# Layer-norm factors folded into the weight splits, early loads in another order and on other queues, compression later

## Chip, cores and metric

The kernel runs on one core of one Trainium2 chip. The metric is the device time of one execution in microseconds (us).

## What is computed

Two layers over 256 tokens of width 1024, in float32. Each layer normalises x by its root mean square with a gain per channel, projects it with one combined matrix, feeds three groups of heads from the result, adds their output projection to x, and then adds a squared-ReLU MLP behind a second norm.

```python
def rms_norm(x, gain):
    y = x * lax.rsqrt(jnp.mean(x * x, -1, keepdims=True) + NORM_EPS) * gain
...
for l in range(DEPTH):                                   # 2 layers
    proj = rms_norm(x, ln1_gain[l]) @ w_in[l]            # 1024 -> 2866 columns
    # split into: NSA q, k_cmp, v_cmp, k_slc, v_slc, k_win, v_win, gates; MLA cq, ckv, kpe; retention q, k, v, gate
    o_nsa = nsa_mixer(...)        # 6 heads: compressed, selected and window branch, gated
    o_mla = mla_mixer(...)        # 5 heads, low-rank keys and values
    o_ret = retention_mixer(...)  # 5 heads, two chunks of 128
    x = x + concat(o_nsa, o_mla, o_ret) @ w_out[l]
    h = rms_norm(x, ln2_gain[l])
    x = x + jnp.square(jax.nn.relu(h @ w_up[l])) @ w_down[l]   # width 4096
return rms_norm(x, final_gain)
```

The compressed branch adds position rows to blocks of 32 keys (values), multiplies each flattened block by `cmp_w1` (2048 x 128), applies gelu and multiplies by `cmp_w2`.

## The kernel before

**Products in three passes.** TensorE works on float32r. Every weight and every activation is held as two parts, `hi` (a rounded copy, made by ScalarE, L140) and `lo` (the remainder, made by VectorE, L141), and `mm3` adds three products (L146 to L148). A weight must be loaded, split, and only then multiplied.

**The stream of weights.** Class `Stream` holds all weights in the order of their use, in units of up to 128 x 1024. A unit is loaded by SP into one of `RAW` = 5 raw buffers, then split into one of `SPL` = 5 pairs of `hi` and `lo`. `get` loads up to `LOAD_AHEAD` = 12 units ahead and splits up to `SPLIT_AHEAD` = 4 ahead. The raw buffer is free again when the split is done. The four `w1` units of the compression are used as loaded: they keep their raw buffers until TensorE has read them. `PIECES` says into how many pieces a split is cut; `START_POOL` names two units of the first chunk whose remainders GpSimd makes.

**Order of a layer.** `inproj` projects chunk by chunk: A (gates and the latent vectors of MLA, 434 columns), B2 (k_cmp, v_cmp, k_slc), B1 (queries), B3 (v_slc, k_win, v_win), of 384 columns each, and rq, rk, rg, rv of the retention, 320 each. Each chunk adds 8 slices of 128 channels for 2 tiles of 128 tokens into two accumulators (tag `acc`, two buffers); ScalarE takes them out with the norm's factor per token, `rstd`, a power that GpSimd computes (L194). In the program the compression (`ps_h`, 64 products with `w1`, then gelu and `ps_kc`) stands between B2 and B1. Then come NSA's scores (`ps_s`), values, retention, the output projection (`l_po`) and the MLP (`ps_up`, `l_pd`). The engines' order is laid by a planner from simulated times: `PRIO` moves parts ahead of or behind their place, and loads go wherever they fit into a queue's planned time, so a load for layer 1 can stand in SP's queue early in layer 0.

**The norm.** `norm_half` multiplies half a tile of x by the gain (`xg`; on GpSimd for one tile of tokens, on VectorE for the other, L503; for the first layer behind the transposes, L499), transposes it on TensorE with the identity (in `c0s`) and splits the result into `xT`. Gains for all later norms are rows broadcast to 128 partitions by SP (512 KB each).

**Small loads.** Per layer SP issues two loads of the MLA norms (L363, L364), two of `w2` and sixteen of position rows (L402, L404), and one of the retention gain (L151). The mask array `c1s` (1056 KB) is one load. GpSimd issues a single load, the positions (L181).

Of the kernel before, what the change touches and what calls it, by code (L numbers as in the profile page):

```python
# [7 lines left out]
F32 = mybir.dt.float32  # L8
# [14 lines left out]
# column offsets of the combined input projection  # L23
# [3 lines left out]
# columns of the first constant array  # L27
C_ID, C_INV, N_C0 = 0, 128, 176
# columns of the second one
C_TRI, C_CM, C_VALID, C_BLK, C_DEC, C_FOLD, N_C1 = 0, 384, 416, 417, 801, 2081, 2113  # L30

# units of weights that are held as loaded and as split; units loaded and split ahead of their use
RAW, SPL, LOAD_AHEAD, SPLIT_AHEAD = 5, 5, 12, 4

# the order of the token tiles where the attention ends
TORD = (1, 0)

# products that only raise the tensor engine's clock before the inputs arrive
WARM = 8
# how far ahead of its place in the program the scheduler takes each part of the work  # L40
# [14 lines left out]
def _parts():  # L55
    """2*pi times 2**11 and 2*pi, cut into parts whose products with small integers are exact."""
# [21 lines left out]
def tile_hybrid_trunk(  # L78
# [59 lines left out]
    def split(hi, lo, src, eng=nc.vector):  # L138
        """src = hi + lo, with hi and lo as the tensor engine's one-pass type."""
# [3 lines left out]

    def mm3(o, a, b, start, stop):
        """o += a^T b in three passes of the operands' parts."""
# [7 lines left out]
    # ---------------------------------------------------------------- inputs that stay  # L153
# [7 lines left out]
    def load_gain(key, row):  # L161
        g = p2.tile([P, D], F32, name=f"gain_{key}", tag="gain", bufs=1)
# [3 lines left out]
    g8 = p2.tile([8, P], F32, name="g8", tag="gain", bufs=1)  # L166
    nc.sync.dma_start(c0s, c0)
    nc.sync.dma_start(xs[:, 0, 0:512], xv[:, 0, 0:512])
# [999 lines left out]
```

## Time and profile before

| | |
|---|---|
| time, median of 3 runs | 682.01 us (680.02 to 683.09) |
| span of the profiled execution | 679.9 us |
| TensorE products / weight loads busy | 659.6 us (97%) / 582.3 us (86%) |
| VectorE busy | 426.9 us (63%) |
| ScalarE busy | 378.4 us (56%) |
| GpSimd busy | 67.2 us (10%) |
| mean granted TensorE clock | 0.992 |
| moved | 111.64 MB, 164 GB/s over the span |

The span runs from the first to the last instruction of one profiled execution; the shortest of the three runs is 0.1 us longer, the median 2.1 us. Products are pipelined and their ends are modelled, so TensorE's busy time says that it had work, not that it ran at its peak.

### The profile page before, as it was taken

The numbers are of one execution on the slowest core, as the hardware profiler recorded it, in microseconds if no ns is written. First come the engines' busy times: TensorE is split into PE (matmuls) and PEld (weight loads), VectorE is DVE, ScalarE is ACT, GpSimd is POOL, SyncE is SP. The second block draws the span as 40 slices with busy tenths as digits, with TensorE's granted clock in tenths as the row PEclk, the third lists the DMA queues.
The fourth block names the chain that finished last, engine by engine and source line by source line (L and its number), as shares of the span: only waits on it lengthen the run. The fifth ranks groups of instructions, "written<-read, shape, count | busy, mean of one in ns | idle before, by whom it ended". The sixth has DMA issues, their size and how long they took to land.

```text
span 679.9 us, 11370 instructions
## 1 busy us (share of the span) xinstructions
PE 659.6 (97%) x4151; PEld 582.3 (86%) x4151; DVE 426.9 (63%) x987; ACT 378.4 (56%) x855; POOL 67.2 (10%) x116
## 2 busy tenths in 40 slices
PE   7989999999999999999999999999999999999995
PEld 5978988677989898989889998876698898989894
DVE  6755867776755555555585597677685555555554
ACT  5856776363745454545466786636284545454542
POOL 3420401201000000000023132111100000000000
PEclk9998899999999999999999999999999999999998
DMA  7897634222865656565647584331285655555511
GB/s 225 254 194 238 176 108 118 71 63 94 281 188 165 208 169 212 166 208 174 180 128 200 168 244 133 93 94 42 83 270 182 199 179 195 185 188 185 186 63 62
DMA packets 79512, 111.64 MB, mean 164 GB/s; under 512 B 9432, under 2 KB 67680, under 8 KB 79328
## 3 DMA queue, kind: packets, MB, share of 16 engines
q1 hardware_dynamic: 79424, 110.92, 53.1%
q8 instruction: 32, 0.52, 0.3%
q14 instruction: 24, 0.20, 0.1%
q0 software_dynamic: 32, 0.00, 0.0%
HBM read 109.86 MB, written 1.05 MB: 163 GB/s over the span
## 4 chain that ended last, share of the span: by engine, by line
PE 88%; DMA 5%; DVE 3%; ACT 2%; issue 1%; SPq 0%; POOL 0%; POOLq 0%; ACTq 0%
PE ps_up L146 9%; PE ps_up L147 9%; PE ps_up L148 9%; PE l_pd L147 8%; PE l_pd L148 8%; PE l_pd L146 8%; DMA raw_B<-in_w_in_dram 3%; PE l_po L146 2%; PE l_po L148 2%; PE l_po L147 2%; PE l_oT L855 2%; PE ps_pT L863 1%; PE ps_s L146 1%; PE l_B L146 1%; DMA raw_rk<-in_w_in_dram 1%; PE l_B L147 1%
## 5 line engine op out<-in xcount | busy, mean ns | idle before, releaser
L141 DVE TENSOR_TENSOR lo_wd<-raw_wd,hi_wd 128x1024 fp32r<-128x1024 f32 x64 | 78.2, 1225 | 111.3 <-ACT hi_wd L140 111.1
L146 PE MATMUL ps_up<-xT,lo_wu 128*128 128x256 f32 x512 | 144.9, 283 | 1.3 <-ACT xT L140 1.3
L147 PE MATMUL ps_up<-xT,hi_wu 128*128 128x256 f32 x512 | 144.9, 283 | 0.0
L148 PE MATMUL ps_up<-xT,hi_wu 128*128 128x256 f32 x512 | 144.1, 282 | 0.0
L140 ACT CAST hi_wd<-raw_wd 128x1024 fp32r<-128x1024 f32 x64 | 67.1, 1051 | 113.7 <-PE l_pd L148 68.0
L148 PE MATMUL l_pd<-hi_wd,u_h 128*128 128x512 f32 x256 | 100.2, 391 | 0.0
L147 PE MATMUL l_pd<-lo_wd,u_h 128*128 128x512 f32 x256 | 100.1, 391 | 0.0
L146 PE MATMUL l_pd<-hi_wd,u_l 128*128 128x512 f32 x256 | 99.7, 389 | 0.0
L140 ACT CAST hi_wu<-raw_wu 128x512 fp32r<-128x512 f32 x128 | 72.6, 618 | 46.3 <-PE ps_up L148 39.0
L146 PEld LDWEIGHTS ps_up<-xT,lo_wu 128*128 128x128 f32 x512 | 96.0, 187 | 2.8 <-ACT xT L140 1.8
L147 PEld LDWEIGHTS ps_up<-xT,hi_wu 128*128 128x128 f32 x512 | 96.3, 188 | 1.4 <-DVE xT L141 0.4
L148 PEld LDWEIGHTS ps_up<-xT,hi_wu 128*128 128x128 f32 x512 | 97.1, 190 | 0.0
L141 DVE TENSOR_TENSOR lo_wu<-raw_wu,hi_wu 128x512 fp32r<-128x512 f32 x128 | 82.1, 685 | 24.0 <-ACT hi_wu L140 23.9
L148 PEld LDWEIGHTS l_pd<-hi_wd,u_h 128*128 128x128 f32 x256 | 48.0, 188 | 10.1
L147 PEld LDWEIGHTS l_pd<-lo_wd,u_h 128*128 128x128 f32 x256 | 48.0, 188 | 9.5
L146 PEld LDWEIGHTS l_pd<-hi_wd,u_l 128*128 128x128 f32 x256 | 48.1, 188 | 9.4
L141 DVE TENSOR_TENSOR lo_B<-raw_B,hi_B 128x192 fp32r<-128x192 f32 (+1 forms) x80 | 28.7, 414 | 24.4 <-ACT hi_B L140 24.2
L146 PE MATMUL l_B<-hi_B,xT 128*128 128x384 f32 x96 | 33.1, 353 | 2.8 <-ACT q_sb L569 2.8
L140 ACT CAST hi_B<-raw_B 128x192 fp32r<-128x192 f32 (+1 forms) x80 | 25.1, 381 | 18.9 <-DMA raw_B<-in_w_in_dram 14.4
L148 PE MATMUL l_B<-hi_B,xT 128*128 128x384 f32 x96 | 32.6, 340 | 0.0
L147 PE MATMUL l_B<-lo_B,xT 128*128 128x384 f32 x96 | 32.5, 339 | 0.0
L819 ACT ACTIVATE p_nsa<-p_nsa,nsa_m 128x256 f32<-128x256 f32 (+2 forms) x72 | 28.4, 397 | 3.3 <-DVE nsa_m L817 3.0
(322 smaller groups left out, 1252.0 us busy)
## 6 DMA issues: line engine op xcount, KB each, us to landing
raw_wu<-in_w_up_dram SPq DMA_DIRECT2D x64, 512.0 KB, 4.6
raw_wd<-in_w_down_dram SPq DMA_DIRECT2D x64, 512.0 KB, 4.2
raw_B<-in_w_in_dram SPq DMA_DIRECT2D x24, 384.0 KB, 3.7
raw_wo<-in_w_out_dram SPq DMA_DIRECT2D x10, 512.0 KB, 3.7
raw_A<-in_w_in_dram SPq DMA_DIRECT2D x8, 434.0 KB, 5.1
raw_wo<-in_w_out_dram SPq DMA_DIRECT2D x12, 256.0 KB, 3.7
raw_w<-in_cmp_w_k_dram SPq DMA_DIRECT2D x8, 256.0 KB, 6.4
raw_w<-in_cmp_w_v_dram SPq DMA_DIRECT2D x8, 256.0 KB, 6.1
```

What stands on the lines that cost most here:

```text
L140: a = nc.scalar.copy(out=hi, in_=src)
L141: b = eng.tensor_tensor(lo, src, hi.bitcast(F32), op=ALU.subtract)
L146: nc.tensor.matmul(o, a[1], b[0], start=start, stop=False)
L147: nc.tensor.matmul(o, a[0], b[1], start=False, stop=False)
L148: nc.tensor.matmul(o, a[0], b[0], start=False, stop=stop)
L819: nc.scalar.activation(p[:, o:o + n], p[:, o:o + n], AF.Exp, scale=-1.0, bias=ms[:, r, b:b + 1], accum_out=ls[:, r, b:b + 1])
L855: nc.tensor.matmul(oT[gp, 0:384], kv_sb[kt][:, vi, gp], pTs[g][:, 0:384], start=i == 0, stop=False)
L863: last = nc.tensor.transpose(ps[:, r * P:(r + 1) * P], prs[g][:, r, o:o + P], ident)
```

## The change

- The gains of both norms are no longer multiplied into x. All four rows of gains are loaded once (`g32`), transposed to one column per slice of 128 channels (`gT`), and multiplied into the weights while these are split: `split_gain` makes `hi` by a ScalarE activation with a factor per partition and `lo` by one VectorE instruction with two operations. Since the factor changes with the slice of channels, each split is cut by slices: 8 pieces a chunk of `w_in`, 4 pieces of 256 columns a unit of `w_up` (before: 2 of 512). `norm_half` keeps the transposes and the split of x. The three broadcast loads of gains go; the final gain is loaded behind the last weights.
- The constants and `g32` are loaded on ScalarE's queue; SP loads the left halves of both tiles of x, then two units of A, then the right halves. B2's first unit comes ahead of the MLA weights.
- The MLA norms, `w2`, the position rows and the retention gain are loaded on GpSimd's queue. The mask array comes in two loads.
- The compression (its products and the loads of `w1`) stands behind rq, and rq ahead of NSA.
- GpSimd no longer splits weights, the rotary tables stand behind chunk A, and `RAW` is 6.

```diff
-RAW, SPL, LOAD_AHEAD, SPLIT_AHEAD = 5, 5, 12, 4
+RAW, SPL, LOAD_AHEAD, SPLIT_AHEAD = 6, 5, 12, 4
...
-PIECES = {'A': 2, 'B1': 4, 'B2': 2, 'B3': 4, 'rk': 2, 'rg': 4, 'rv': 2, 'wo': 2, 'wu': 2}
-START_POOL = (1, 2)
+PIECES = {'wo': 2}
...
+    def split_gain(hi, lo, src, g):
+        nc.scalar.activation(hi, src, AF.Copy, scale=g)
+        nc.vector.scalar_tensor_tensor(lo, in0=src, scalar=g, in1=hi.bitcast(F32), op0=ALU.mult, op1=ALU.subtract)
...
-        g = p2.tile([P, D], F32, name=f"gain_{key}", tag="gain", bufs=1)
+        g = p1.tile([P, D], F32, name=f"gain_{key}", tag="mid")
...
-    nc.sync.dma_start(c0s, c0)
-    nc.sync.dma_start(xs[:, 0, 0:512], xv[:, 0, 0:512])
-    nc.sync.dma_start(g8, ln1_gain[0].rearrange("(k p) -> k p", p=P))
-    nc.sync.dma_start(xs[:, 0, 512:D], xv[:, 0, 512:D])
+    g32 = p2.tile([32, P], F32, name="g32", tag="h_sb", bufs=1)
+    nc.scalar.dma_start(c0s, c0)
+    nc.scalar.dma_start(g32[0:16], ln1_gain.rearrange("l (k p) -> (l k) p", p=P))
+    nc.scalar.dma_start(g32[16:32], ln2_gain.rearrange("l (k p) -> (l k) p", p=P))
+    for t in range(2):
+        nc.sync.dma_start(xs[:, t, 0:512], xv[:, t, 0:512])
...
     def late_start():
-        nc.sync.dma_start(xs[:, 1, :], xv[:, 1, :])
+        for t in range(2):
+            nc.sync.dma_start(xs[:, t, 512:D], xv[:, t, 512:D])
...
+            if parts:
+                for g, a, b in parts:
+                    split_gain(p[0][:, a:b], p[1][:, a:b], raw[:, a:b], gT[:, g:g + 1])
+                return p
...
-                     nc.gpsimd if (l, name) == (0, "A") and i in START_POOL else nc.vector)
+                     [(8 * l + k, j * n, (j + 1) * n) for j, k in enumerate(ks)])
...
-            nc.sync.dma_start(nrm[:, 0:2], mla_q_norm[l].rearrange("(k p) -> p k", p=P))
-            nc.sync.dma_start(nrm[:, 2:3], mla_kv_norm[l].rearrange("(k p) -> p k", p=P))
+            nc.gpsimd.dma_start(nrm[:, 0:2], mla_q_norm[l].rearrange("(k p) -> p k", p=P))
+            nc.gpsimd.dma_start(nrm[:, 2:3], mla_kv_norm[l].rearrange("(k p) -> p k", p=P))
...
-                nc.sync.dma_start(w2s[:, z], w2[l])
+                nc.gpsimd.dma_start(w2s[:, z], w2[l])
                 for rep in range(8):
-                    nc.sync.dma_start(pos_t[rep * 16:(rep + 1) * 16, z], pe[l].rearrange("(b a) d -> a b d", b=2))
+                    nc.gpsimd.dma_start(pos_t[rep * 16:(rep + 1) * 16, z], pe[l].rearrange("(b a) d -> a b d", b=2))
...
-                                    wuv[:, 4 * i:4 * i + 4, c * 256:(c + 1) * 256])], 1024)
+                                    wuv[:, 4 * i:4 * i + 4, c * 256:(c + 1) * 256])], 1024,
+                 [(16 + 8 * l + 4 * i + k, k * 256, (k + 1) * 256) for k in range(4)])
...
-        bcast_row(gng, ret_gn_gain[l].rearrange("h d -> (h d)"), 320)
+        nc.gpsimd.dma_start(gng, ret_gn_gain[l].rearrange("h d -> (h d)").unsqueeze(0).broadcast_to([P, 320]))
...
+    def masks(a, b):
+        def load():
+            nc.sync.dma_start(c1s[:, a:b], c1[:, a:b])
+        return load
...
         if l == 0:
-            add_chunk(l, "A", 1)
+            add_chunk(l, "A", 2)
             W.add("x1", late_start)
-            add_chunk(l, "A", 4, 1)
+            add_chunk(l, "A", 4, 2)
         else:
             add_chunk(l, "A")
+        add_chunk(l, "B2", 1)
         add_mla(l)
-        add_chunk(l, "B2")
+        add_chunk(l, "B2", 4, 1)
         add_cmp(l)
         if l == 0:
-            W.add("c1", lambda: nc.sync.dma_start(c1s, c1) and None)
+            W.add("c1a", masks(0, C_DEC))
         add_chunk(l, "B1")
-        add_w1(l)
         add_chunk(l, "B3")
         add_chunk(l, "rq")
+        if l == 0:
+            W.add("c1b", masks(C_DEC, N_C1))
+        add_w1(l)
         add_chunk(l, "rk")
...
-        gain_unit(l, f"b{l}", ln2_gain[l])
...
-        if l + 1 < DEPTH:
-            gain_unit(l, f"a{l + 1}", ln1_gain[l + 1])
-        else:
-            gain_unit(l, "f", final_gain)
...
+        if l + 1 == DEPTH:
+            add_side(l, "gain_f", lambda: load_gain("f", final_gain))
...
-    def norm_half(t, h, gain, eng=nc.vector):
+    def norm_half(t, h):
         ps = wk("ps_xT", "MN"[h])
...
-        eng.tensor_tensor(xg, xs[:, t, sl], gain[:, sl], op=ALU.mult)
         for j in range(4):
-            nc.tensor.transpose(ps[:, j * P:(j + 1) * P], xg[:, j * P:(j + 1) * P], ident)
+            nc.tensor.transpose(ps[:, j * P:(j + 1) * P], xs[:, t, h * 512 + j * P:h * 512 + (j + 1) * P], ident)
...
+    ps_g = acc("ps_g")
+    nc.tensor.transpose(ps_g[:, 0:32], g32, ident[0:32, 0:32])
+    nc.vector.tensor_copy(gT, ps_g[:, 0:32])
...
-            for t in range(2):
-                for h in range(2):
-                    last = norm_half(t, h, None)
+            for h in range(2):
+                for t in range(2):
+                    last = norm_half(t, h)
...
-        if l == 0:
-            rope_tables()
...
         inproj("A", evac_a)
+        if l == 0:
+            rope_tables()
...
         inproj("B2", evac_b2)
+        inproj("B1", evac_b1)
+        inproj("B3", evac_b3)
+        inproj("rq", evac_rope(rq, "rq", nc.gpsimd))
         with prio("h"):
             psh = wk("ps_h")
...
-        inproj("B1", evac_b1)
-        inproj("B3", evac_b3)
...
-        inproj("rq", evac_rope(rq, "rq", nc.gpsimd))
         inproj("rk", evac_rope(rk, "rk", nc.vector))
```

## Rows read from the trace of the kernel before

**Rows 1.** Waits of TensorE: who waited for whom, us in total, times, longest.

```profile
PE l_rq L146 <- ACT l_kv L569: 2.8, 2, 2.1
...
PE l_B L146 <- ACT q_sb L569: 2.8, 1, 2.8
...
PE ps_up L146 <- ACT xT L140: 1.3, 2, 0.7
...
PE l_A L146 <- DVE xT L141: 1.1, 1, 1.1
...
PE ps_xT L505 <- DVE xg L503: 0.5, 1, 0.5
...
PE l_A L147 <- POOL lo_A L141: 0.3, 1, 0.3
```

**Rows 2.** Busy time by stretch: PE, PEld, DVE, ACT, POOL, granted clock, DMA share, GB/s.

```profile
50.90:54.40 3.50, 3.44 (x18) 2.88 (x22) 1.54 (x8) 2.55 (x8) 0.00 (x0) 0.61 0.47 124
...
69.00:72.50 3.50, 3.49 (x14) 3.49 (x15) 3.12 (x13) 3.03 (x10) 2.24 (x9) 0.55 0.72 229
...
166.50:344.00 177.50, 177.50 (x1142) 162.28 (x1142) 103.91 (x139) 90.50 (x141) 0.87 (x1) 1.00 0.60 191
...
390.00:490.70 100.70, 99.71 (x599) 80.42 (x598) 74.12 (x256) 61.12 (x190) 18.11 (x27) 1.00 0.39 120
```

**Rows 3.** Timeline of the start, all engines: start, us, engine, what; idle time before.

```profile
8.25 0.91 ACT L140 CAST hi_A<-raw_A 128x868 fp32r<-128x868 f32 x1 [6.23 <-DMA raw_A<-in_w_in_dram]
...
11.24 0.71 PE L146 MATMUL l_A<-hi_A,xT 128*128 128x434 f32 x1
...
11.79 4.59 POOL L141 TENSOR_TENSOR lo_A<-raw_A,hi_A 128x868 fp32r<-128x868 f32 x2 [9.45 <-ACT hi_A L140]
...
14.39 2.54 DVE L141 TENSOR_TENSOR xT<-xg,xT 128x512 fp32r<-128x512 f32 x1
...
19.01 0.98 POOL L194 TENSOR_TENSOR l_rstd<-l_ms,mhalf 128x1 f32<-128x1 f32 x1 [2.63 <-DVE l_ms L515]
```

**Rows 4.** Groups by line and form, ScalarE, then VectorE: count; busy us, mean ns; idle before.

```profile
L140 ACT CAST hi_wu<-raw_wu 128x512 fp32r<-128x512 f32 x128 | 72.6, 618 | 46.3 <-PE ps_up L148 39.0 <-PE l_pd L148 6.3 <-DVE lo_wu L141 0.9
...
L388 ACT ACTIVATE hi_uq<-raw_uq,l_nrm 128x480 fp32r<-128x480 f32 x4 | 2.7, 691 | 0.0
...
L600 ACT ACTIVATE junkm<-l_a 128x256 f32<-128x256 f32 x4 | 1.6, 412 | 0.0
...
L141 DVE TENSOR_TENSOR lo_wu<-raw_wu,hi_wu 128x512 fp32r<-128x512 f32 x128 | 82.1, 685 | 24.0 <-ACT hi_wu L140 23.9
...
L389 DVE SCALAR_TENSOR_TENSOR lo_uq<-raw_uq,l_nrm,hi_uq 128x480 fp32r<-128x480 f32 x4 | 2.8, 708 | 0.0
```

**Rows 5.** Timeline of SP's queue in layer 0, 22 to 70 us.

```profile
31.89 4.57 SPq L415 DMA_DIRECT2D raw_w<-in_cmp_w_k_dram  x4
...
42.40 1.02 SPq L323 DMA_DIRECT2D raw_B<-in_w_in_dram  x1
...
50.89 0.39 SPq L323 DMA_DIRECT2D raw_B<-in_w_in_dram  x1
```

**Rows 6.** Timeline of TensorE, layer 0, then layer 1 around the compression.

```profile
54.32 2.29 PE L730 MATMUL ps_h<-raw_w,l_T 128*32 128x128 f32 x64
...
384.03 1.98 PE L730 MATMUL ps_h<-raw_w,l_T 128*32 128x128 f32 x64
...
402.08 0.29 PE L752 MATMUL ps_kc<-g,l_w2s 128*64 128x16 f32 x4
...
404.90 0.31 PE L148 MATMUL l_rq<-hi_rq,xT 128*128 128x320 f32 x1
...
411.95 0.39 PE L146 MATMUL ps_s<-l_kT,l_qT 64*128 64x272 f32 x1
```

**Rows 7.** Instructions of line 181, the one load that GpSimd issues: ns min/median/max.

```profile
L181 POOL DMA_DIRECT2D pos_i<-in_positions_dram x1: 959/959/959, 1.2 to 1.2; - x1
...
DMA to landing us min/median/max: 4.7/4.7/4.7
```

More of the change, by code (lines that the diff above doesn't have):

```diff
@@ L314, in hilo, with add_unit @@
         return [splitp.tile([P, 1024], F32R, name=f"{z}_{name}", tag=z) for z in ("hi", "lo")]
-    def add_unit(key, pieces, n, eng=nc.vector):
+    def add_unit(key, pieces, n, parts=None):
         name = "_".join(str(z) for z in key)
@@ L327, in split_ @@
             p = hilo(name)
-            m = n // PIECES.get('A0' if key[:2] == (0, 'A') else key[1], 1)
+            if parts:
+                for g, a, b in parts:
+                    split_gain(p[0][:, a:b], p[1][:, a:b], raw[:, a:b], gT[:, g:g + 1])
+                return p
+            m = n // PIECES.get(key[1], 1)
             for o in range(0, n, m):
-                split(p[0][:, o:o + m], p[1][:, o:o + m], raw[:, o:o + m], eng)
+                split(p[0][:, o:o + m], p[1][:, o:o + m], raw[:, o:o + m])
             return p
@@ L386, in f @@
                 for k, a, b in parts:
[L387 to L395 removed]
+                    split_gain(p[0][:, a:b], p[1][:, a:b], raw[:, a:b], nrm[:, k:k + 1])
+                return p
+            return f
+        W.add((l, "uq"), load_uq, split_lat(f"uq{l}", ((0, 0, 480), (1, 480, 960))))
+        W.add((l, "uk"), load_uk, split_lat(f"uk{l}", ((2, 0, 640),)))
     def add_cmp(l):
@@ L720, in tile_hybrid_trunk, with evac_b1, evac_b3, evac_rope @@
         inproj("B2", evac_b2)
+        qT = [p1.tile([P, 3, S], F32R, name=f"{L}qT{i}", tag=f"qT{i}") for i in range(2)]
+        kv_sb = [None, None]
+        def evac_b1(t, ps):
+            q = scr("q_sb", [P, 3, 2, 64])
+            scaled(q.rearrange("p r g d -> p g r d"), ps.rearrange("p (g r d) -> p g r d", g=2, r=3), t)
+            qv = q.rearrange("p r g d -> p (r g) d")
+            rope(nc.vector, qv[:, :, 0:16], t, 0, 8, qv[:, :, 0:16], (6,))
+            ps2 = wk("ps_qT")
+            for r in range(3):
+                nc.tensor.transpose(ps2[:, r * P:(r + 1) * P], q[:, r].rearrange("p g d -> p (g d)"), ident)
+            split(qT[0][:, :, t * P:(t + 1) * P], qT[1][:, :, t * P:(t + 1) * P],
+                  ps2[:, 0:384].rearrange("p (r c) -> p r c", r=3))
+        def evac_b3(t, ps):
+            kv = p1.tile([P, 3, P], F32, name=f"{L}kv{t}", tag=f"kv{t}")
+            kv_sb[t] = kv
+            scaled(kv.rearrange("p a d -> p (a d)"), ps, t)
+            X = kv[:, 1].rearrange("p (g d) -> p g d", g=2)[:, :, 0:16]
+            rope(nc.gpsimd, X, t, 0, 8, X, (2,))
+            ps2 = wk("ps_kwT")
+            nc.tensor.transpose(ps2[:, 0:P], kv[:, 1], ident)
+            o = 272 + t * P
+            split(kT[0][:, o:o + P], kT[1][:, o:o + P], ps2[:, 0:P])
+        inproj("B1", evac_b1)
+        inproj("B3", evac_b3)
+        rq, rk, rv, gs = [None] * 2, [None] * 2, [None] * 2, [None] * 2
+        def evac_rope(lst, nm, eng):
+            def f(t, ps):
+                z = scr(f"{L}{nm}{t}", [P, 5, 64], chain="M")
+                scaled(z.rearrange("p h d -> p (h d)"), ps, t)
+                rope(eng, z, t, 48, 32, z, (5,))
+                lst[t] = z.rearrange("p h d -> p (h d)")
+            return f
+        inproj("rq", evac_rope(rq, "rq", nc.gpsimd))
         with prio("h"):
@@ L1002, in tile_hybrid_trunk @@
                 with prio("norm"):
-                    last = norm_half(t, h, gains[f"b{l}"], nc.gpsimd if t == TORD[0] else nc.vector)
+                    last = norm_half(t, h)
         W.release(last, SPLIT_AHEAD)
@@ L1067, in tile_hybrid_trunk @@
                 with prio("norm"):
-                    last = norm_half(t, h, gains[f"a{l + 1}"], nc.gpsimd if t == 0 else nc.vector)
+                    last = norm_half(t, h)
         W.release(last, SPLIT_AHEAD)
```

55 lines of the change are left out of this document (2 added, 53 removed).

## The prediction

> **What bounds the kernel now.** The table above has TensorE busy for 97% of the span, so its order of work sets the time, and only what leaves it idle or slows its clock can be won back. The first view is therefore the list of what TensorE waited for [rows 1]. Apart from the start, where x has to arrive in either kernel, it holds a handful of stalls: one of 2.8 us in front of chunk B1, two in front of rq (2.8 together, the longer 2.1, so the other is 0.7), two of about 0.67 where the first product of the MLP waits for the transposed norm, 1.1 + 0.3 in chunk A, 0.5 at the turn to the second layer. The second view, the busy times by stretch [rows 2], then shows two more things. After each of the two long stalls of layer 0 the granted clock is down: 0.61 over 50.9 to 54.4 and 0.55 over 69.0 to 72.5, a mixture of the 1.2 and the 2.4 GHz level. And the MLP, 177.5 us long, is TensorE without a gap, with ScalarE busy for 90.5 and VectorE for 103.9. The MLP, over half of the span with its second pass, can therefore only be lost in, not won in.
>
> **The start.** The third view is the timeline. The first product of chunk A runs at 11.24 [rows 3]. Its first weights are there at 8.25 (ScalarE sat idle for them until then); VectorE then has rotary tables, gain products and the remainders of the splits in one queue. GpSimd's splits of two units (4.59 together) overlap a VectorE subtraction of 512 columns that takes 2.54, where one of that width takes 0.69 by the groups of like form [rows 4]. The change takes these things out of the way: the four gain products, GpSimd's splits, and the tables, which go behind A. It also loads the two left halves of x first, then A's first two units. The first unit of A is third on SP's queue in place of fifth, but the bytes ahead of it are the same two halves of x and the constants, so it lands between 7.4 (two issues of 0.4 earlier, [rows 5]) and 8.25. Then one scaled piece of 434 columns on ScalarE: a scaled copy of 480 columns takes 0.69, a plain cast of 512 takes 0.62 [rows 4], so some 0.65. The factors must be there by then: three loads on ScalarE's queue, a transpose and a copy, at 0.4 an issue and in the time in which ScalarE idles; without that idle time 1.2. First product at 8.1 to 8.9; I take 8.8, a gain of 2.4. The two waits inside A, 1.4, have lost both their causes (GpSimd's remainder, the late VectorE subtraction), but ScalarE now has eight scaled pieces in place of four wide ones and GpSimd has loads to issue (below), so of the 3.8 I take 3.0; bounds 0 and 3.8.
>
> **Compression later, and a sixth raw buffer.** This is the large term. SP starts loading the four w1 tiles at 31.89 [rows 5]. They aren't split; each sits in a raw buffer until the h products at 54.32 [rows 6]. Four of five buffers are thus taken and B1 and B3 come through one: single loads at 42.40 and 50.89. That is the 2.8 stall, and the rq stall behind it. With w1 loaded behind rq, and h behind rq, w1 finds its input T long ready, so it is held only as long as it loads; and there is one buffer more. What goes with the stalls: 2.8 + 2.1 = 4.9 idle, and the clock, (1 - 0.61) x 3.5 + (1 - 0.55) x 3.5 = 2.9. Together 7.8; layer 1, whose loads run further ahead, still shows one stall of 0.7 at rq, so I leave two such and take 6.4. Bounds: 0 (the next load is late instead: rk, which now stands behind w1) and 7.8. In layer 1 the same order takes up to 0.7; I take 0.5.
>
> **No gain product at the norms.** The product stands between the sum and the transposes. At either entry to the MLP the transposes can then go in among the last output products, and the 0.67 goes; at the turn to layer 1 the 0.5. I take 1.8. Below that nothing, if the transposes stay behind the products anyway; above it 3.2, if VectorE's two products of 512 columns (0.7 each, as wide as those of [rows 4]) also leave the queue in front of chunk A. The three broadcast loads of gains fall away from SP; none was waited for.
>
> **Gains in the splits.** The same number of elements is written; the form and the pieces change. w_in has 8 pieces for each of 8 chunks, 64 a layer, against 71 and 75 before: no more than now. w_up has 4 pieces of 256 a unit instead of 2 of 512. The trace has no scaled copy of 256 columns from SBUF with a factor per partition, so: not under 0.41 (256 columns without such a factor), not over 0.69 (480 columns with it) [rows 4]. For 32 units a layer against 2 x 0.618 that adds 13 to 49 us to ScalarE's 90.5; nearer the lower end, as the width is the same. VectorE's new form takes 0.708 for 480 columns, so between half of that and all of it for 256, against 2 x 0.685: 1.5 to 47 us on 103.9. Both stay under the MLP's 177.5 even at the upper ends (139 and 151), and TensorE's other work covers them: I price them at 0. Were the cover gone, what exceeds 177.5 would be paid twice.
>
> **Small loads on GpSimd's queue.** 21 a layer (18 of the compression, 2 norms, 1 retention gain). SP loses their issue time, but in TensorE's list no wait ends on SP, and I have put the late loads down to buffers, not to the queue; gain 0. GpSimd pays. The one load there today occupies it for 0.96 and lands after 4.7 [rows 7]. Twenty in front of layer 0's work, at 0.96, are 19.2, from 2.2 to 21.4; the norm's power (0.98, [rows 3]), which every evacuation of A waits for, would in the worst order end at 22.4, against an end of A's products near 21: 1.4. Bounds: 0 and 1.4 at this price; at 4.7 each, if a load held the queue until it landed, A would wait until 96, but in the row the two times differ, so the queue is free long before. It is inside the 0.8 that I held back above. Queued behind them stand the power, then the rotary keys of MLA, for which TensorE has B2 and B1 as cover; the 21 of layer 1 wait until layer 0's copies have been read, and the rotations of k_win and rq stand behind them, wanted only by the attention. The Trainium skill (DMA: Bandwidth & Descriptors, Anatomy of one DMA) speaks of about 50 ns of dispatch and a small, variable time to make descriptors; by it the twenty would take about 1 us of queue, an estimate, and nothing could be late. The 0.96 of the trace differs, and I go by it. Mask loads cut in two, final gain at the end: 0; nothing waits there now.
>
> **The sum.** 3.0 + 6.4 + 0.5 + 1.8 = 11.7. The profiled span is 679.9, so 668.2. The median of the runs shown is 682.01, 2.1 above that span; on that footing 670.3, say **670**. With all terms at their upper bounds (15.5) it is 666.5, with half of them 676; so 664 to 676 is the forecast's own range.
>
> **Rivals.**
> *The stalls only move.* B1 is on time, but rk and rg, now behind w1, aren't, and the clock falls there in place of here. For: w1 still takes four of six buffers at a stretch. Against: the h products follow at once. Then the start, the norms and nothing else: 682 - 3.0 - 1.8 = 677.
> *Late compression holds up the attention.* It ends on the other side. In layer 1 the first product of the compressed keys comes 18.0 us behind the first h product (384.03 to 402.08), and the first NSA scores at 411.95 [rows 6]. With h behind the last rq product (404.90), the same 18 give 422.95: scores 11 us later. NSA ends last in each layer, its softmax lies on VectorE and ScalarE, and rk, rg, rv then have been used up as cover. If all 11 came out as idle TensorE, two layers cost 22: 670 + 22 = 692. If half, 681. It decides from 5.9 a layer on (11.7 over two). Against: from 390 to 490.7 TensorE is busy for 99.7 of 100.7 [rows 2], so it is the bound there and retention and output products can be taken forward; for: its weight loads are busy for only 80, so the products aren't packed.
> *GpSimd's queue jams.* If the twenty loads cost 1.5 us and all stand before the norm's power, A's evacuation comes at 33 and B2, which needs A's two accumulators, with it: 12 us, the whole gain, 682. At 0.96 it's 672, inside the forecast.
> *The splits of w_up bind.* Only if both ends above were exceeded; 682 or more.
>
> **Chances.** Forecast 0.58; stalls move 0.14; compression late by about half 0.09, by more 0.11; jam 0.05 (0.03 of it same); splits 0.03. Changes under 0.5% (3.4 us) can't be told from none here. Faster: 0.58 + 0.14 = 0.72; same: 0.09 + 0.03 = 0.12; slower: 0.11 + 0.02 + 0.03 = 0.16. For 8 in 10, the range goes down past the sum of the upper bounds to 662 and up through the moved stalls and the half-late compression to 683; the far ends of the late compression and of the jam stay out.
>
> **What would show it.** Right: first product of A before 9.5 and chunk A over by 22; no stall over 1 us in front of B1 or rq, granted clock 1.00 from 24 to 160; MLP of layer 0 in full work by 156 (now 166.5, [rows 2]); no wait for the transposed norm at either MLP; each MLP still 177 to 178. Wrong: a wait of an evacuation for GpSimd's power near 20; TensorE idle in front of ps_s or l_oT (late compression); waits in front of rk or rg for their loads; products of ps_up waiting for a split. I would be wrong most cheaply on the order in which the planner now lays the attention, which the profile of before can't show.

## The result, and the profile after

The changed kernel takes 687.75 us (median of 4 runs, 683.42 to 690.15) beside 681.46 of the kernel before on the same chip: ratio 1.0102 [1.0057, 1.0147]. Forecast were 670. The profiled execution is the fastest of the four: span 681.6, mean granted clock 0.991; the other three have spans of 685.8 to 688.3 at a clock of 0.978 to 0.985. So 1.7 us of the loss stand in the profile (681.6 against 679.9), and the rest comes with a lower granted clock: span times mean clock is 673 to 676 us in all four.

What TensorE waited for in the changed kernel (us in total, times, longest), to be laid beside [rows 1]:

```profile
PE l_po L149 <- DVE l_mixT L139: 4.1, 4, 1.4
PE l_A L149 <- DVE xT L139: 3.2, 1, 3.2
PE ps_cT L598 <- ACT l_a L567: 3.0, 1, 3.0
PE l_rg L149 <- ACT l_rk L567: 1.5, 1, 1.5
PE ps_hT L778 <- ACT h_sb L775: 1.2, 1, 1.2
...
PE ps_pT L876 <- DVE nsa_m L830: 0.9, 1, 0.9
PE ps_xT L502 <- DVE xs L1004: 0.7, 2, 0.3
PE ps_s L149 <- DVE nsa_m L830: 0.7, 2, 0.4
...
PE ps_up L150 <- DVE xT L139: 0.6, 2, 0.3
```

The stalls in front of B1 and rq are gone, as forecast, and others have come: one in front of the transposes of A's latents (`ps_cT`), and a row of them that end on the attention's vector work (`mixT`, `nsa_m`) or on evacuations. One, before the transposes of h (`ps_hT`), is a step of the compression itself, in layer 1. The busy times of three of the stretches of [rows 2] (us; busy time and count of TensorE, its weight loads, VectorE, ScalarE, GpSimd; then granted clock, DMA share, GB/s):

```profile
50.90:54.40 3.50, 3.50 (x23) 3.50 (x22) 2.14 (x5) 3.46 (x9) 3.50 (x8) 1.00 0.80 166
69.00:72.50 3.50, 2.99 (x21) 2.62 (x19) 1.05 (x3) 1.50 (x4) 2.74 (x4) 1.00 0.76 213
166.50:344.00 177.50, 177.22 (x1141) 162.00 (x1140) 115.22 (x201) 108.40 (x203) 0.00 (x0) 1.00 0.62 186
```

The clock in the first two of these stretches, 0.61 and 0.55 before, is 1.00 now, and the MLP is as full as it was. Along TensorE's order of work:

```profile
68.22 0.31 PE L151 MATMUL l_rq<-hi_rq,xT 128*128 128x320 f32 x1
...
73.42 1.99 PE L772 MATMUL ps_h<-raw_w,l_T 128*32 128x128 f32 x64
...
97.61 0.39 PE L149 MATMUL ps_s<-l_kT,l_qT 64*128 64x272 f32 x1
```

rq is over at 68.5 (78.6 before). Of these 10.0 us, 2.3 are the h products, which now come behind. The first NSA scores start at 97.6 (84.8 before), and the MLP's first product at 166.3 (165.1 before): what stood 10.0 ahead at rq stands 1.2 behind at the MLP. Layer 1 repeats it smaller: 144.1 us from its first product of A to its MLP in place of 143.4. The two MLPs give back 0.85 and 0.35; the last 1.0 of the 1.7 us lies behind the last product, which the end of the program follows 8.5 us later in place of 7.5.

### The profile page after: what moved, and what is told of

It reads as the page before. It is cut to its first block, busy times and chain, and to the rows that moved or that the text cites. A ratio compares the mean times of both kernels' runs of the same rounds, so it can differ in the third digit from the quotient of the medians.

```text
span 681.6 us, 11568 instructions
## 1 busy us (share of the span) xinstructions
PE 654.4 (96%) x4151; PEld 579.8 (85%) x4151; DVE 448.5 (66%) x1089; ACT 420.9 (62%) x965; POOL 75.7 (11%) x150
## 4 chain that ended last, share of the span: by engine, by line
PE 84%; DMA 5%; DVE 5%; ACT 4%; issue 1%; SPq 0%; POOL 0%; POOLq 0%; ACTq 0%
PE ps_up L150 9%; PE ps_up L151 9%; PE ps_up L149 9%; PE l_pd L150 9%; PE l_pd L151 9%; PE l_pd L149 8%; DMA raw_rk<-in_w_in_dram 2%; PE l_po L149 2%; PE l_B L149 2%; PE l_B L150 2%; PE l_B L151 2%; PE l_po L150 2%; PE l_po L151 2%; PE l_oT L868 2%; DMA xs<-in_x_dram 1%; PE ps_pT L876 1%
## 5 line engine op out<-in xcount | busy, mean ns | idle before, releaser
L144 ACT ACTIVATE hi_wu<-raw_wu,gT 128x256 fp32r<-128x256 f32 x256 | 109.0, 498 | 28.9 <-PE ps_up L151 23.6
L145 DVE SCALAR_TENSOR_TENSOR lo_wu<-raw_wu,gT,hi_wu 128x256 fp32r<-128x256 f32 x256 | 107.2, 480 | 9.9 <-ACT hi_wu L144 9.9
L145 DVE SCALAR_TENSOR_TENSOR lo_B<-raw_B,gT,hi_B 128x384 fp32r<-128x384 f32 x48 | 28.3, 632 | 11.7 <-ACT hi_B L144 11.6
L144 ACT ACTIVATE hi_B<-raw_B,gT 128x384 fp32r<-128x384 f32 x48 | 26.4, 609 | 8.2 <-PE ps_uq L151 5.0
```

Source lines behind the costliest of these rows:

```text
L144: nc.scalar.activation(hi, src, AF.Copy, scale=g)
L145: nc.vector.scalar_tensor_tensor(lo, in0=src, scalar=g, in1=hi.bitcast(F32), op0=ALU.mult, op1=ALU.subtract)
```

## The experiments

All times are ratios to the kernel before, run on the same chip, with 95% intervals; 1% is 6.8 us. "Layer 0 ends" is the first product of its MLP, in the profile. A run is named by its short label (e2, f1) behind the words that say what it is.

### Where the compression stands

**Compression back in its old place** (e2). The block from h to the compressed keys goes back between B2 and B1, the w1 loads between B1 and B3, and the masks' second half (the fold matrix is in it) to the first.

```
         add_chunk(l, "B1")
+        add_w1(l)
         add_chunk(l, "B3")
         add_chunk(l, "rq")
-        add_w1(l)
...
         inproj("B2", evac_b2)
+        with prio("h"):
+            psh = wk("ps_h")
...
```

> The changed kernel with the compression (h, its gelu, the compressed keys) at its old place between B2 and B1, its tiles w1 loaded between B1 and B3 again, the second half of the masks loaded with the first (the fold matrix is in it). Theory A (the late compression holds up the NSA attention; what the projections gained is given back behind them): the first NSA scores of layer 0 come 8 to 13 us earlier than at 97.6, the waits before l_po (2.9 in layer 0) go, and the time falls by 6 to 10, to 678 to 682 us. Rival B (the order of the compression does not matter, the loss lies in the splits with gains and in the start): within 2 us of 687.75, with the stalls before B1 and rq back.

Measured 673.2 us, 0.9907 [0.9892, 0.9923]: 13 us under the changed kernel, and faster than the kernel before too; no complete kernel of this study is clearly faster (f1 and f4 below can't be told from it). Scores from 83.1, layer 0 ends at 160.8. Its waits on TensorE:

```profile
PE l_A L149 <- DVE xT L139: 4.3, 1, 4.3
PE ps_cT L597 <- ACT l_a L566: 2.6, 1, 2.6
PE l_po L149 <- DVE l_mixT L139: 2.4, 2, 1.2
...
PE l_rq L149 <- ACT l_kv L566: 1.1, 2, 0.8
```

The start is as bad as in the changed kernel; the stalls in front of B1 and rq do not come back, and those of the attention shrink. By the profiles 9.1 us lie between the two kernels: 5.5 in layer 0, 2.7 in layer 1 (141.4 from its first product of A to its MLP, in place of 144.1) and 0.9 behind the last product; the rest of the 13 goes with the lower granted clock of the changed kernel's other executions. So the one part of the change that I had priced highest as a gain is the one that loses.

**The kernel before with the compression late, and nothing else** (e4).

```
-        add_w1(l)
         add_chunk(l, "B3")
         add_chunk(l, "rq")
+        add_w1(l)
...
+        inproj("rq", evac_rope(rq, "rq", nc.gpsimd))
         with prio("h"):
...
```

> The kernel before with only the order changed: chunks B1, B3 and rq in front of the compression, w1 loaded behind rq. Five raw buffers and the old splits stay. Theory A (late compression gives the gain back in the attention): projections through rq end 6 to 10 us earlier than 78.6, the first scores 8 to 13 us later than 84.9, time 681 to 688. Rival B (late compression is a gain, the loss is elsewhere): 673 to 676.

1.0065 [1.0043, 1.0086]. The projections through rq end 13.5 us earlier (65.1), layer 0 1.2 later (166.3), layer 1 takes 147.9 in place of 143.4. The first scores come only 2.8 later, not the 8 to 13 that theory A wanted. The loss belongs to the late place, with the old splits as with the new ones.

### Small loads, buffers, start

**Small loads back on SyncE**, in the changed kernel and with the compression early (e1 and e3; `nc.gpsimd.dma_start` of `nrm`, `w2s`, `pos_t`, `gng` becomes `nc.sync.dma_start`).

> The changed kernel with its 21 small loads a layer on SyncE's queue again, nothing else. Theory 1 (the loads in front of the norm's power on GpSimd, and the splits that ScalarE then has in front of A's evacuation, make the 3.0 us wait in front of the transposes of A's latents): that wait falls under 0.5 and the time by about 3, to some 684.5 us against 687.75 of the changed kernel. Theory 2 (the wait is only ScalarE's order, or work that is needed anyway): under 1 us. Theory 3 (SyncE now pays: 21 x 0.42 us of issue in front of the weights of B2 and B1): slower by up to 9, 690 or more.

> Both edits at once: compression at its old place and small loads on SyncE's queue. If the two costs are separate and both real: 9 to 13 us under the changed kernel, 675 to 679, so faster than the kernel before (681.5) by the new start, the sixth buffer and the norms. If neither is real: 687.

Late, 1.0098 [1.0085, 1.0111]: no difference, though the wait in front of the latents' transposes falls from 3.0 to 1.0. Early, 0.9990 [0.9978, 1.0001], 5.5 us slower than with the loads on GpSimd: TensorE waits 5.9 in one place in front of B, where ScalarE has a split of a B unit, 6.2 us late from memory, ahead of B2's evacuation. So the move to GpSimd is worth 5.5 us where the compression is early, and nothing where it is late.

**The move alone, in the kernel before** (g3), where small loads stand between the single loads of [rows 5] on SyncE's queue:

```profile
43.77 2.50 SPq L404 DMA_DIRECT2D l_pos_t<-in_cmp_pos_k_dram  x5
```

> The kernel before with one part of the change alone: its 21 small loads a layer (two norms, eighteen of the compression, the retention's gain) on GpSimd's queue in place of SyncE's. The prediction priced this at 0, since TensorE showed no wait for SyncE. Theory S (the small loads, two of which wait until layer 0's copies are read, keep the loads of B1, B3 and rq back on SyncE; e3 against e2: 5.5 us): the waits in front of B1 and rq shrink by half or more, ratio 0.990 to 0.995. Theory R (five raw buffers alone make these waits): ratio 0.998 to 1.002. If GpSimd is late with the norm's power: 1.003 or more.

1.0044 [1.0029, 1.0059]. What TensorE waited for:

```profile
PE ps_xT L492 <- DMA xs<-in_x_dram: 4.4, 2, 3.0
PE l_A L147 <- POOL lo_A L141: 3.6, 1, 3.6
...
PE l_rq L146 <- ACT l_kv L569: 1.1, 2, 0.6
```

The stall of 2.8 before B1 is gone and rq's fell from 2.8 to 1.1, with five buffers and the compression early. That fits theory S, but does not show it: chunk B starts 6.9 us later here (31.1 in place of 24.3), behind the wait for GpSimd's remainder of A listed above, and rq ends where it did (78.7, before 78.6), so the late start alone may have hidden the stalls. Theory S's ratio, 0.990 to 0.995, missed. What separates the two is e3 beside f1 below, with six buffers both and B started within 0.1 us in both: with the loads on SyncE the stall of 5.9 is there and layer 0 ends at 164.4, with them on GpSimd it is not and layer 0 ends at 160.1.

**Five buffers in place of six**, early and late (f2 and g6; `RAW` 6 to 5).

> e2_cmp_early with five raw buffers in place of six. If the early stalls before B1 and rq are a matter of buffers, as the prediction had it, they come back (2.8 and 2.1 us, and the clock falls): 5 to 8 us slower, ratio 0.998 to 1.003. If they came from the small loads on SyncE's queue instead: under 2 us, ratio 0.990 to 0.994.

> The changed kernel with five raw buffers in place of six. If the late place of the compression already frees the buffers for B1 and rq, as the prediction had it: within 2 us of the changed kernel, ratio 1.008 to 1.013. If the sixth buffer carries it there as it does in the early place (f2 against e2, 6.5 us): 1.015 to 1.022.

Early 1.0012 [0.9999, 1.0025], 6.5 us slower than with six; the waits before rq are 4.3 in place of 1.1. The longer one is in layer 1:

```profile
393.93 0.41 PE L149 MATMUL l_rq<-hi_rq,xT 128*128 128x320 f32 x1 [2.94 <-ACT l_kv L566]
```

In layer 0 no stall comes back before B1, rq waits 1.35 (e2 0.8), and the layer ends at 160.4, as in e2 (160.8). Of the 4.5 us between the profiles, 3.9 are in layer 1. So the stalls of layer 0 that the prediction put down to the buffers do not return with five of them; B starts 0.7 us later than in e2 (27.6), which may hide a part. Late 1.0117 [1.0087, 1.0147], as the changed kernel: the late place makes no use of the sixth.

**Two mends of the start**, both on e2: the power ahead of the small loads (f1), and the rotary tables behind the norm of x (f4).

```
+            with (tc.issue_after(power[-1]) if l == 0 else nullcontext()):
                 for z, (pe, w2) in enumerate(...):
                     nc.gpsimd.dma_start(w2s[:, z], w2[l])
...
         if l == 0:
+            with tc.issue_after(last[1].ins):
-            rope_tables()
+                rope_tables()
```

> The kernel with the compression back at its old place (e2_cmp_early, 0.9907 of the kernel before), and layer 0's eighteen small loads of the compression issued on GpSimd's queue behind the norm's power. Theory 1 (the loads ahead of the power let the planner put A's evacuation behind nine splits on ScalarE): the wait in front of the transposes of A's latents, 2.6 us there, falls under 1, ratio 0.987 to 0.989. Theory 2 (the evacuation's place on ScalarE has nothing to do with GpSimd's queue): the wait stays, ratio 0.990 to 0.992. Against both: the encodings of the positions come later, and the input of h with them.

> e2_cmp_early with the rotary tables issued behind the last subtraction of x's norm. Theory 1 (VectorE works on the tables from 6.6 to 9.0 us, so the copy of the factors and with it A's first split wait): first product of A at 7.5 to 8.6 in place of 10.5, time 1 to 2.5 us less, ratio 0.987 to 0.989. Theory 2 (x's right halves, there from 10 to 11 us on, bound chunk A anyway): first product earlier, but A ends where it did, at 22.9; ratio 0.990 to 0.992.

Both do what they should where they act. With the power first, the wait for A's evacuation is 0.4 and B starts at 24.5 in place of 26.9; with the tables late, the first product of A runs at 7.2 in place of 10.5, x's right halves are then waited for (4.1), and B starts no earlier (27.6). Neither is worth anything at the end: 0.9913 [0.9895, 0.9932] and 0.9923 [0.9906, 0.9941]. With the power first, 1.7 of the 2.4 us are lost again before rq, in waits in front of chunk B and of MLA's transposes; ScalarE waits 2.5 us there for B's weights.

### Why the late place costs

**The attention does not read the compressed keys and values** (f3).

```
+        for z in kT:
+            nc.vector.tensor_scalar(z[:, 256:272], ident[:, 0:16], 0.0, None, op0=ALU.mult)
...
-            split(kT[0][:, 256:272], kT[1][:, 256:272], kc_)
+            split(kx[0], kx[1], kc_)
```

> The changed kernel, compression late, with one thing left out: the NSA scores and values read zeros and the bare block mask in place of the compressed keys and values. The compression is still computed up to the split of its keys (one product of 384 columns on VectorE becomes a copy), in the same late place and with the same loads. Theory A (what costs is that the attention has to wait for late compressed keys): the scores start 10 us or more earlier than at 97.6 and the time falls to e2's, ratio 0.988 to 0.996. Rival C (what costs is the place of the w1 loads ahead of rk, rg, rv, or that the projections are used up before the attention whatever the keys do): ratio 1.005 to 1.012.

1.0150 [1.0117, 1.0182]: theory A falls as it stood, and the ratio lies above the rival's range as well. TensorE's order of work there:

```profile
78.78 1.99 PE L776 MATMUL ps_h<-raw_w,l_T 128*32 128x128 f32 x64 [1.50 <-DVE l_kT L139]
...
86.88 0.77 PE L782 MATMUL ps_hT<-c1s,h_sb 128*128 128x32 f32 x4 [2.86 <-ACT h_sb L779]
...
97.67 0.29 PE L798 MATMUL ps_kc<-g,l_w2s 128*64 128x16 f32 x2
97.89 0.39 PE L149 MATMUL ps_s<-l_kT,l_qT 64*128 64x272 f32 x1
```

The scores read nothing of the compression and still start 0.2 us behind its last product. So f3 frees the keys, but does not test an early start of the attention. TensorE itself stands for the compression's steps, 1.5 and 2.9 us; the 2.9 is in part a late load, since ScalarE's copy of h stood behind a split of rv that had waited 2.4 us for memory.

**The attention first, the compression behind it** (g2), and **the compression half way**, behind B3 (g5):

> As f3_keys_free (zeros and the bare mask in place of the compressed keys and values), with the whole compression issued behind the NSA attention of its layer. In f3 the scores started at 97.9, with the compression's last product at 97.7, although they read nothing of it: they take the same two PSUM banks, in the order of the program. Here nothing of the compression stands ahead of them on those banks. Theory A, mended (what costs is that the scores start late, by keys or by banks; then the attention's softmax ends last with little beside it): the first scores of layer 0 at 80 to 86 in place of 97.9, the layer's MLP starts at 158 to 162 in place of 170, ratio 0.985 to 0.995 against 1.015. Rival C (the projections, finished early, leave the attention without cover wherever it starts; or the w1 loads ahead of rk, rg, rv cost): ratio 1.005 or more.

> The changed kernel with the compression half way: behind chunk B3 and in front of rq, w1 loaded between B3 and rq. Theory A, mended: time follows the start of the scores, which the program's order now puts among rg's products (rk's with the compression early, rv's with it late): scores at 88 to 93, ratio between the two, 0.994 to 1.004. Rival C or a cost of the w1 loads: as the changed kernel, 1.008 or more, or as the early place, 0.992 or less.

1.0824 [1.0782, 1.0867] and 1.0171 [1.0144, 1.0198]; the numbers of theory A miss in both; those of the rivals (1.005 or more, 1.008 or more) hold, the first far above. In g2 the scores start at 78.7, but the retention, behind the compression in the program, ends last: layer 0 ends at 190.6. That says what the retention costs when it stands last, and nothing on the start of the scores. In g5 the scores start at 99.1, later than with the compression behind rq, and TensorE waits 1.9 in front of rq in layer 0 and 2.1 in front of rk in layer 1, chunks whose weights are loaded behind w1 there. Part of its loss is the start, with B 2.9 us later than in the changed kernel: in the profiled execution the positions landed at 9.7, and A's first product waited until 13.2.

**No compression at all** (k5), and **late compression with MLA's attention taken forward** (k1; `'mla': 0` to 1600, `'mlat': -300` to 800):

> The changed kernel with the compression left out: no h products, no gelu, no compressed keys and values (zeros and the bare mask in their places, as in f3), no loads of w1. Early and late compression are then the same kernel. The work left out is some 3.2 us of TensorE a layer (h 2.0, its transposes 0.5, keys and values 0.7), 6.4 in all. Theory A: the compression costs its own 6 us when early and 20 when late, so 0.979 to 0.985 (665 to 669). Theory C (it is the projections that run ahead of the attention; the early compression slows them and so keeps cover): the order without it is as bad as with it late, less its own work: 0.998 to 1.004.

> The changed kernel, compression late, with two offsets of the planner changed: MLA's attention is taken 1600 places ahead in place of 0, its softmax 800 ahead in place of 300 behind. Nothing else. The planned order then has MLA's scores among rq's products and the projections rg and rv between the NSA scores, where the changed kernel has all of rk, rg and most of rv in front of them. Theory C (with the compression late the planner runs the projections dense and early, so that the two attentions, bound by VectorE and ScalarE, start behind them and end the layer without cover): ratio to the kernel before 0.990 to 1.000, MLP of layer 0 starting at 158 to 163, waits behind 100 us as few as with the early compression (2.3 us; 6.5 in the changed kernel). Theory A (the late compressed keys themselves hold the end): scores no earlier than 95, ratio 1.006 to 1.013.

0.9855 [0.9832, 0.9879] without it, at the end of theory A's range. By the ratios the compression costs 3.5 us when early and 16.8 when late. Theory C, that the projections run ahead of the attention whatever the compression does, is out as the main cause. Taking MLA forward gives 1.0075 [1.0048, 1.0103], 1.8 us of some 13, its interval overlapping that of the changed kernel.

One thing that most late kernels share is seen in the busy times of 60 to 100 us (columns as above). The changed kernel, then e2, then the kernel without compression, then f3:

```profile
60.00:80.00 20.00, 19.49 (x181) 18.64 (x180) 10.04 (x23) 11.18 (x29) 6.68 (x13) 1.00 0.71 182
80.00:100.00 20.00, 18.54 (x132) 17.13 (x131) 19.05 (x63) 15.29 (x44) 4.00 (x6) 1.00 0.80 248
```

```profile
60.00:80.00 20.00, 19.18 (x127) 18.35 (x126) 14.73 (x42) 15.81 (x44) 7.05 (x16) 1.00 0.77 242
```

```profile
60.00:80.00 20.00, 20.00 (x129) 18.83 (x128) 15.13 (x41) 14.84 (x38) 6.74 (x13) 1.00 0.54 160
```

```profile
60.00:80.00 20.00, 18.15 (x156) 17.36 (x158) 10.98 (x26) 11.77 (x30) 6.85 (x13) 1.00 0.71 163
```

VectorE is busy for 10 to 11 of these 20 us in the two late kernels shown (8.5 to 11.9 in e1, e4, g2, g5 and g6) and for 14.7 and 15.1 in e2 and k5 (16.0 in the kernel before; 13.4 and 19.0 in e3 and f2); the changed kernel then has it full, 19.05 of 20, in the next 20. The rule has exceptions: k1, late, has 14.1 at a ratio of 1.0075, and k3 (below), early, 15.3 at 1.0121. Two lists say what was missing: SyncE's loads in the changed kernel, and what ScalarE waited for from 55 to 100 us.

```profile
50.22 2.69 SPq L422 DMA_DIRECT2D raw_w<-in_cmp_w_k_dram  x4
53.00 4.17 SPq L422 DMA_DIRECT2D raw_w<-in_cmp_w_v_dram  x4
59.93 8.23 SPq L329 DMA_DIRECT2D raw_rk<-in_w_in_dram  x3
69.18 7.53 SPq L329 DMA_DIRECT2D raw_rg<-in_w_in_dram  x3
```

```profile
ACT hi_rk L144 <- DMA raw_rk<-in_w_in_dram: 5.7, 2, 3.6
...
ACT hi_rg L144 <- DMA raw_rg<-in_w_in_dram: 1.5, 1, 1.5
ACT hi_rv L144 <- DMA raw_rv<-in_w_in_dram: 1.2, 2, 0.9
```

w1's four tiles take their raw buffers from 50.2 on and keep them until the h products at 73.4 to 75.4. The loads of rk and rg come through the two that are left, at 59.9 to 67.8 and 69.2 to 76.3 (in e2 rg's first load is issued at 61.5). ScalarE waits 8.4 us for rk, rg and rv, VectorE behind it; the work comes in a heap at 80 to 100, evacuations and softmax late with it. In layer 1 these waits are 4.7.

Two runs speak against this hold as the whole cause. In g6, with five buffers, one is left beside w1, rk's loads drag on much longer, and ScalarE waits 11.4 us for rk and rg; yet the time is that of the changed kernel.

```profile
63.60 14.61 SPq L329 DMA_DIRECT2D raw_rk<-in_w_in_dram  x3
```

In k1 ScalarE waits only 2.1 us for these loads, and yet no more than 1.8 of the 13 us come back.

**The compression in a PSUM bank of its own**, with the real keys and without (m3 and m2; `wk("ps_h")`, `wk("ps_hT")`, `wk("ps_kc")` become `att(f"{L}ps_h", "N")` and so on):

> The changed kernel, compression late and complete; only its three results (h, its transposes, the compressed keys and values) stand in the PSUM bank in which NSA's values are summed later, in place of the two banks that they share with q's and k's transposes and with NSA's scores. Theory B (late, the compression holds those two banks in the order of the program, from h to the last product of its keys 17 us, and whatever of the NSA comes behind it waits): ratio 0.990 to 0.998, MLP of layer 0 at 159 to 163 in place of 166. Theory K (it isn't the banks but the late keys, or the compression's steps between other work on TensorE, ScalarE and VectorE): ratio 1.006 to 1.014, MLP at 165 to 168.

> The same bank, and the NSA reads zeros and the bare mask in place of the compressed keys and values, as in f3 (1.015): neither keys nor banks hold the scores any more, the work of the compression stays, late. Theory B: as fast as m3 or faster, 0.985 to 0.995, first scores at 76 to 84. If m3 is slow and this one fast, it is the late keys; if both are slow, it is the compression's steps among the rest in late place, 1.005 or more.

1.0459 [1.0439, 1.0480] and 1.0428 [1.0404, 1.0452]: 24 and 22 us slower than the changed kernel, by something that neither theory had. With a bank free, the planner put the h products singly between those of rq:

```profile
69.19 0.41 PE L149 MATMUL l_rq<-hi_rq,xT 128*128 128x320 f32 x1
69.53 0.43 PE L772 MATMUL l_ps_h<-raw_w,l_T 128*32 128x128 f32 x2
69.90 0.41 PE L150 MATMUL l_rq<-lo_rq,xT 128*128 128x320 f32 x1
```

No idle time is listed, but one product of rq and two of h come every 0.71 us here; in a row, a product of rq comes every 0.147 and the 64 products of h take 1.99 together, so the three take 0.21. In layer 1 of m3, rq and h take 23.0 us with 56 changes from the one to the other, in the changed kernel 9.1 with none: 0.25 us a change. Those 13.9 us are most of the 15.4 by which layer 1 is longer than in the changed kernel. So the two runs say nothing on banks or keys.

### Trying for more

Both start from e2 and take MLA's attention forward, in k2 by the offsets of k1, in k3 by 400 places with its softmax at 0.

> e2_cmp_early with the same two offsets. If the order of the attention against the projections is what counts, and e2 has it right already: within 0.3% of e2 (0.9907), a little better if the last waits (l_po 1.2 a layer) go. If MLA taken forward costs the NSA its place: slower, 0.995 or more.

> e2_cmp_early with MLA's attention 400 places ahead and its softmax at 0: in the planned order the NSA scores stand among rk and rv and the transposes of its first tile among rv. By theory C the more projections are kept beside the attention, the better: 0.983 to 0.990. If e2 is at the limit of TensorE's work: 0.989 to 0.993.

1.0022 [1.0008, 1.0036] and 1.0121 [1.0095, 1.0147]: slower than e2 by 8 and 15 us. In k2 the waits listed for TensorE are no longer than in e2, but the tile that it works for changes 158 times between A and the MLP of layer 0, in e2 133 times. The count alone decides nothing, since k5, the fastest, has 149. e2 stays the best, with f1 and f4 level: the change without its late compression.

## Why the prediction was wrong, step by step

**The start** (+3.0 taken, bounds 0 and 3.8): below its lower bound. B's first product comes 1.9 us later than before.

```profile
6.60 0.17 DVE L210 CAST pos_f<-pos_i 128x2 f32<-128x2 int32 x1 [5.60 <-DMA pos_i<-in_positions_dram]
...
8.98 0.18 DVE L524 COPY gT<-ps_g 128x32 f32<-128x32 f32 x1
...
10.03 0.44 PE L149 MATMUL l_A<-hi_A,xT 128*128 128x434 f32 x1 [3.24 <-DVE xT L139]
...
15.29 0.16 DVE L512 SCALAR_TENSOR_TENSOR l_ms<-l_ss 128x1 f32<-128x1 f32 x1 [0.54 <-ACT junk L508]
...
19.01 1.12 POOL L200 TENSOR_TENSOR l_rstd<-l_ms,mhalf 128x1 f32<-128x1 f32 x2
...
23.25 2.12 ACT L144 ACTIVATE hi_B<-raw_B,gT 128x384 fp32r<-128x384 f32 x4
25.28 1.12 ACT L567 ACTIVATE l_a<-l_A,l_rstd 128x434 f32<-128x434 f32 x2
25.94 0.44 PE L598 MATMUL ps_cT<-c0s,l_a 128*128 128x128 f32 x2 [3.04 <-ACT l_a L567]
```

Two steps failed. That "the factors must be there by then" hides VectorE: the tables moved behind A in the program only, the planner ran them as soon as the positions had landed (6.6), and the copy of the factors stands behind them; first product 10.03, not 8.8. And the 0.8 held back for GpSimd did not hold: the power came at 19.0 with its input there at 15.4, and on ScalarE nine pieces of later splits stood in front of A's evacuation, which ran at 25.3 though the power was done at 20.1. This is the jam that I gave 0.05, by way of ScalarE's order. f4 and f1 showed both causes, and that neither decides the end: most of what the start wins is lost again by rq.

**Compression later** (+6.9): the early stalls and the clock went as said. The step that failed is that w1 "is held only as long as it loads": issued from 50.2, it was held until 75.4, longer than in [rows 5, 6], now in front of rk and rg. My lower bound, "the next load is late instead: rk", was the case, but it did not stop at 0: with the attention behind it, the late place costs some 13 us, 4.4 in the kernel before. The rival "Late compression holds up the attention", given 0.20 in all, came near the size, "about half" of its 22 us; its mechanism, late keys, is not borne out (f3). "The stalls only move", given 0.14, came true in small: waits of 0.5 and 1.5 in front of rk and rg.

**Sixth buffer** (inside the same 6.9): it is worth 6.5 us, and only with the compression early (f2, g6), but mostly in layer 1. The step "four of five buffers are thus taken … that is the 2.8 stall" is not borne out: with five buffers and the small loads on GpSimd that stall is not there (f2), with six and the loads on SyncE one of 5.9 is (e3).

**No gain product** (+1.8): 0.65. The waits at the norms were 0.67, 0.68 and 0.54; now the transposes wait 0.34 for the sum and a product behind the first one 0.28 for the remainder, at either MLP, and nothing at the layer's turn. Taking away the product leaves its neighbours in the chain.

**Gains in the splits** (0): right.

```profile
L144 ACT ACTIVATE hi_wu<-raw_wu,gT 128x256 fp32r<-128x256 f32 x256 | 109.0, 498 | 28.9 <-PE ps_up L151 23.6
L145 DVE SCALAR_TENSOR_TENSOR lo_wu<-raw_wu,gT,hi_wu 128x256 fp32r<-128x256 f32 x256 | 107.2, 480 | 9.9 <-ACT hi_wu L144 9.9
```

498 ns lies in the bounds of 410 to 690, 480 in those of 354 to 708; ScalarE is busy for 108.4 of the MLP's 177.5 us, VectorE for 115.2, and no product waits for a split.

**Small loads** (0): wrong on both sides. "No wait ends on SP" did not show that the queue costs nothing: the waits stood under a buffer's or an evacuation's name. In e2 the move is worth 5.5 us, in g3 most of the stalls that I had put down to buffers are gone with it. On GpSimd a load that was moved took 0.50 to 0.74, not 0.96. The Trainium skill (DMA: Bandwidth & Descriptors, Anatomy of one DMA) gives about 50 ns for dispatch alone and only "small, variable" for making the descriptors. The measured time is ten times that dispatch, so my estimate of about 1 us for the twenty was far too low; the measured value decides.

**What stays open.** Shown is that the late place costs some 13 us, that freeing the keys alone gives nothing back, and that without compression, w1 and all, nothing of it is left. That w1's hold on the raw buffers is a main part agrees with the loads, with VectorE's busy time in most late kernels, and with g5's waits; g6 and k1 speak against it as the whole, and no run moved w1 alone or gave it buffers of its own, so it is argued, not shown. The start of the scores does not explain it either: they start at 89.9 in e1 and at 87.7 in e4, at 97.6 in the changed kernel, and the loss is there in all three. The steps of the compression on TensorE's queue have a share (4.4 us in f3, 1.2 in the changed kernel's own profile); whether the finer order of work has another, no run shows.

The rest of the difference between the median and the profile goes with the clock. In e1, a late kernel whose profiled span of 684.7 is near its median, TensorE had waits and loose work behind 100 us, and the granted clock fell behind them, to a mixture of 1.2 and 2.4 GHz:

```profile
100.00:108.00 8.00, 7.22 (x57) 5.83 (x57) 6.36 (x25) 7.12 (x24) 0.00 (x0) 1.00 0.67 181
108.00:120.00 12.00, 12.00 (x58) 8.84 (x57) 6.24 (x29) 5.82 (x25) 0.00 (x0) 0.72 0.16 44
```

## What to carry to other kernels

When a buffer's holder is moved, follow it to its new place: ask which loads stand behind it there, and who works on them, before the stall it leaves is booked as a gain. A step moved in the program of a planned kernel is not moved on its engine; the copy, the evacuation or the power that is wanted first can stand behind ready work in an in-order queue. And time won in a stage that ends on loads need not be won: two mends of the start took 2 to 3 us out of it and nothing off the end that shows. Before a stall is put down to too few buffers, change their number and nothing else: f2 was that run, and in layer 0 the stall did not come back.

## What was not expected of the hardware

Changing on TensorE between the h products (results on 32 partitions, fp32) and those of rq costs about 0.25 us a change, which the trace counts as busy time: 13.9 us over 56 changes in layer 1 of m3. Which of the two, the place of the results or the type, makes it, no run shows. An order that fills every gap can lose more than the gaps.

GpSimd's queue of loads stands still at times for the landing of a load issued eight places earlier, before it issues the next (the changed kernel):

```profile
4.10 2.05 POOL L411 DMA_DIRECT2D l_pos_t<-in_cmp_pos_k_dram  x4
6.85 0.50 POOL L411 DMA_DIRECT2D l_pos_t<-in_cmp_pos_k_dram  x1 [0.71 <-DMA pos_i<-in_positions_dram]
9.46 0.50 POOL L411 DMA_DIRECT2D l_pos_t<-in_cmp_pos_k_dram  x1 [2.10 <-DMA l_nrm<-in_mla_q_norm_dram]
```

The ninth load waits for the first, the positions; the tenth for the second. Each load is cheap at 0.5 us, but a late landing among them holds whatever computes on GpSimd behind. In e2 the same two waits are 1.19 and 0.90. Whether the chip sets the distance of eight or the program's own semaphores, no run shows.
